# Down products of a hybrid encoder block by Strassen over two blocks and three parts of K, with operands made ahead in DRAM

## The chip, the cores and the metric

The kernel runs on one core of a Trainium2 chip. TensorE (PE) multiplies, VectorE (DVE) and ScalarE (ACT) do the elementwise work, GpSimd (POOL) mostly starts DMAs here, and SyncE (SP) starts the other DMAs. The metric is the device time of one execution in microseconds (us). The profile is a recording of one execution.

## The reference

One layer of an encoder over 2048 tokens of 1024 channels. The part that matters here is the SwiGLU at the end and the last norm:

```python
x = x + jnp.concatenate([y_a, y_b.astype(y_a.dtype)], axis=-1) @ w_out[l]
h2 = rmsnorm(x, norm2_g[l])
x = x + (jax.nn.silu(h2 @ w_gate[l]) * (h2 @ w_up[l])) @ w_down[l]
return rmsnorm(x, final_norm_g)
```

w_gate and w_up are 1024 x 2816, w_down is 2816 x 1024, everything is float32. Ahead of it stand the projections, gated linear attention in both directions, a gMLP mixer and the output projection.

## The kernel before

Activations lie as channels x tokens: 128 partitions of one channel block by 512 tokens (a block b, four of them, TB = 512). A float32 product is made of three fast ones: each operand is split into a high half, rounded by a cast on ScalarE, and a low half, the difference, on VectorE; then high x high, high x low and low x high are summed in PSUM. In program text the halves end in h and l.

The gate and up products already use the Winograd form of Strassen's method: two blocks of tokens (a pair, `PAIRS`: blocks 3 and 2, then 1 and 0), two output tiles of 128 channels (a step p, 11 of them for gate and 11 for up) and two halves of K form a 2x2 problem, done in seven products of 4 x 3 matmuls instead of eight. The seven moving operands (`slots`) are made once per pair by `moving` and `put`; the seven stationary ones are made from the raw weights for each step p by `Stationary.job`: sums of quarters of the weight on L343, a cast on L361, the low half on L362. `Stream` makes them four products ahead. `STEADY` is the order of the seven products; `quarter` is called when one of the four output tiles is complete. For gate it applies tanh on ScalarE (L968) and a product on VectorE (L969); for up it multiplies with the gate (L980) and GpSimd writes the result to DRAM (`da`, L981).

The down stage, from L1008 on, is not in that form. For each of the four blocks it loads 22 blocks of w_down (`wdn`, 512 KB each, in every block again) and 22 of the activations (`ar`), splits both (L1038, L1039 and `split`), and sums 22 x 3 products into each of 8 output tiles (`pd`, on L110 to L112). After a block the residual is added (L1097), the squares are summed, one wide sum over channels (L197) and its root give the norm, and the scaled block leaves from GpSimd's queue (L1050, L1053). The last block is done in two half columns, so that the first half's norm lies beside the second half's products; its outputs leave from SP's queue (L1107, L1110).

Instructions are written in program order, but a scheduler of the framework then sets the order on each engine from its own estimates, and may draw an instruction ahead of others of the same engine. Buffers are tiles of pools: a new tile waits until the one in its place has been read. Every engine works through its own instructions strictly in that order; a waiting instruction holds those behind it.

Of the kernel before, what the change touches and what calls it, by code (L numbers as in the profile page):

```python
# [8 lines left out]
F32 = mybir.dt.float32  # L9
# [5 lines left out]
P = 128  # L15
T = 2048
D = 1024
# [10 lines left out]
def encoder_block(  # L28
# [22 lines left out]
    wdn: bass.AP,  # L51
# [174 lines left out]
    def put(i, src):  # L226
# [3 lines left out]
        for k in range(0, HK, 2):  # L230
            c = slice(k, k + 2)
            nc.scalar.copy(out=hi[:, c, :], in_=src[:, c, :])
            nc.vector.tensor_tensor(out=lo[:, c, :], in0=src[:, c, :], in1=hi[:, c, :].bitcast(F32), op=ALU.subtract)
            yield

    def moving(b11, b21, b12, b22):
# [3 lines left out]
        def sub(o, a, b):  # L240
            for k in range(0, HK, 2):
                c = slice(k, k + 2)
# [11 lines left out]
        yield from put(6, b22)  # L254
        yield from sub(b21, b21, b11)
        yield from put(5, b21)

# [4 lines left out]
    d_a = {b: [drp.tile([P, TB], F32, tag=f"da{b}_{j}", name=f"da{b}_{j}") for j in range(NF)] for b in range(NB)}  # L262
# [15 lines left out]
    STEADY = (0, 4, 3, 1, 2, 6, 5)  # L278
# [12 lines left out]

    class Stationary:


        def __init__(self):
# [4 lines left out]
            for n, (i, p, w, o) in enumerate(self.seq):  # L300
                turn = p in (0, 1, NP - 1)
                need = []
                for r in ((0,) if o in (0, 4) else (1,) if o in (3, 5) else (0, 1)):
# [14 lines left out]
            self.stream = Stream([lambda n=n: self.job(n) for n in range(len(self.seq))], ahead=4)  # L318

        def ask(self, done):  # L320

            for x, q in enumerate(self.queues):
                while self.asked[x] < len(q) and (self.asked[x] < 2 or q[self.asked[x] - 2]["last"] < done):
# [5 lines left out]
                    self.asked[x] += 1  # L329

# [556 lines left out]


    psums.close()
    psf = ctx.enter_context(tc.tile_pool(name="psf", bufs=1, space=bass.MemoryType.PSUM))  # L890
    cg = gp.tile([P, 4, TB], F32, tag="g", name="cg")
    with tc.tile_pool(name="pf", bufs=1) as pf:
# [3 lines left out]
        slots.update({i: tuple(pf.tile([P, HK, TB], F32R, tag=f"s{i}{x}", name=f"s{i}{x}") for x in "hl") for i in (2, 5)})  # L896
        s5h, s5l = slots.pop(5)
        homes[6] = lambda: (ps6.tile([P, HK, TB], F32R, tag="w0", name="s6h"), s5l)
        homes[5] = lambda: (s5h, ps6.tile([P, HK, TB], F32R, tag="w1", name="s5l"))
        later = []  # L900

        def flush():
            while later:
                later.pop(0)()

        def seven(quarter, name):

            bank = {}

            def temp(n, bufs=2):  # L910
                return pf.tile([P, TB], F32, tag=n, name=f"{n}{name}", bufs=bufs)

            def product(i, key, start=True):
                whi, wlo = ws.next()
                if start and ops.n <= 5:
                    bank[key] = other(f"{name}{key}")
                elif start:
                    bank[key] = psf.tile([P, TB], F32, tag="sp", name=f"{name}{key}", bufs=7)
                o = bank[key]
                thi, tlo = slots[i]  # L920
                for k in range(HK):
                    c = slice(k * P, (k + 1) * P)
                    f, l = start and k == 0, k == HK - 1
                    nc.tensor.matmul(out=o, lhsT=whi[:, c], rhs=thi[:, k, :], start=f, stop=False, skip_group_check=True)
                    nc.tensor.matmul(out=o, lhsT=whi[:, c], rhs=tlo[:, k, :], start=False, stop=False, skip_group_check=True)
                    nc.tensor.matmul(out=o, lhsT=wlo[:, c], rhs=thi[:, k, :], start=False, stop=l, skip_group_check=True)
                flush()
                return o

            def add(o, a, b):  # L930
                nc.vector.tensor_tensor(out=o, in0=a, in1=b, op=ALU.add)

            def s0():
                st["u2"] = temp("u2", 4)
                nc.scalar.copy(out=st["u2"], in_=product(0, "a"))

            def s1():
                add(st["u2"], product(1, "b"), st["u2"])
# [281 lines left out]
```

## Time and profile before

| | us |
|---|---|
| median of 3 runs | 2120.22 (2115.94 to 2120.43) |
| profiled execution | 2115.95 |
| its span, first to last instruction | 2114.3 |
| TensorE busy | 2084.4 (99%) |
| VectorE busy | 1362.9 (64%) |
| ScalarE busy | 871.6 (41%) |
| GpSimd busy | 169.6 (8%) |

The profile gives for each engine how long it was busy, in slices of the span, in groups of instructions, and as a chain from the last instruction backwards. Matmuls overlap, so that a row's duration (0.39 us) is longer than the distance from one start to the next. The gate and up stage takes the span from about 772 to 1616 us, the down stage the rest.

### The profile page before, as it was taken

The numbers are of one execution on the slowest core, as the hardware profiler recorded it, in microseconds if no ns is written. First come the engines' busy times: TensorE is split into PE (matmuls) and PEld (weight loads), VectorE is DVE, ScalarE is ACT, GpSimd is POOL, SyncE is SP. The second block draws the span as 40 slices with busy tenths as digits, with TensorE's granted clock in tenths as the row PEclk, the third lists the DMA queues.
The fourth block names the chain that finished last, engine by engine and source line by source line (L and its number), as shares of the span: only waits on it lengthen the run. The fifth ranks groups of instructions, "written<-read, shape, count | busy, mean of one in ns | idle before, by whom it ended". The sixth has DMA issues, their size and how long they took to land.

```text
span 2114.3 us, 25808 instructions
## 1 busy us (share of the span) xinstructions
PE 2084.4 (99%) x9728; PEld 1706.6 (81%) x9728; DVE 1362.9 (64%) x2134; ACT 871.6 (41%) x1473; POOL 169.6 (8%) x266
## 2 busy tenths in 40 slices
PE   8999999999999999999999999999999999999998
PEld 6787877888888878888888888888888888888887
DVE  6977666676666768676666976666666355353633
ACT  6765455464646542332233523322324333233321
POOL 0222222010110100000000000000000000000000
PEclk9999999999999999999999999999999999999999
DMA  8633244453543434222222332222225537364531
GB/s 294 204 112 130 95 140 157 138 191 113 199 173 135 149 125 149 85 73 88 80 85 75 126 144 90 73 87 80 85 75 196 170 133 245 128 219 154 175 114 40
DMA packets 94109, 281.42 MB, mean 133 GB/s; under 512 B 11680, under 2 KB 19744, under 8 KB 90784
## 3 DMA queue, kind: packets, MB, share of 16 engines
q1 hardware_dynamic: 79824, 226.81, 31.6%
q0 software_dynamic: 14016, 52.44, 6.7%
q8 instruction: 76, 1.25, 0.2%
q10 hardware_dynamic: 144, 0.52, 0.1%
q14 instruction: 49, 0.40, 0.1%
HBM read 225.20 MB, written 54.53 MB: 132 GB/s over the span
## 4 chain that ended last, share of the span: by engine, by line
PE 91%; DVE 5%; DMA 2%; ACT 2%; issue 1%; SPq 0%; POOL 0%; DVEq 0%; ACTq 0%
PE pd L111 8%; PE pd L112 8%; PE pd L110 8%; PE pout L111 3%; PE pout L112 3%; PE pout L110 3%; PE pu L112 1%; PE pu L110 1%; PE pu L111 1%; PE pg L110 1%; PE pz L110 1%; PE pg L112 1%; PE pg L111 1%; PE pz L111 1%; PE pz L112 1%; PE pv L112 1%
## 5 line engine op out<-in xcount | busy, mean ns | idle before, releaser
L981 POOL DMA_DIRECT2D da<-q x88 | 47.6, 541 | 801.7 <-DVE q L980 768.9
L968 ACT ACTIVATE th<-cg 128x512 f32<-128x512 f32 x66 | 41.5, 631 | 105.5 <-DVE cg L966 97.1
L969 DVE SCALAR_TENSOR_TENSOR cg<-th,cg 128x512 f32<-128x512 f32 x66 | 45.2, 686 | 15.6 <-ACT th L968 15.6
L848 DVE TENSOR_TENSOR xc<-pout,xc 128x512 f32<-128x512 f32 x32 | 21.9, 688 | 44.1 <-PE pout L112 43.9
L980 DVE SCALAR_TENSOR_TENSOR q<-q,cg 128x512 f32<-128x512 f32 x66 | 45.3, 686 | 0.6
L1053 POOL DMA_DIRECT2D out_dram<-xg x12 | 8.6, 717 | 368.3 <-DVE xg L1050 368.3
L545 POOL TENSOR_SCALAR qs<-QK,misc 128x128 f32<-128x128 f32 x30 | 25.6, 857 | 151.8 <-DVE QK L496 77.3
L569 DVE SCALAR_TENSOR_TENSOR sf<-sf,misc,dsb 64x128 f32<-64x128 f32 x56 | 19.9, 355 | 23.3 <-ACT dsb L559 22.7
L744 DVE SCALAR_TENSOR_TENSOR sb<-sb,misc,dsr 128x128 f32<-128x128 f32 x30 | 10.0, 344 | 36.5 <-PE pob L734 35.8
L1038 ACT CAST a_8h<-ar 128x512 fp32r<-128x512 f32 x32 | 18.7, 618 | 19.0 <-DMA ar<-da 18.9
L552 ACT COPY ot<-po 128x256 f32<-128x256 f32 x32 | 10.3, 374 | 38.6 <-PE po L549 21.9
L1125 DVE TENSOR_TENSOR xg<-pd,xg 128x256 f32<-128x256 f32 x16 | 6.8, 425 | 28.2 <-PE pd L112 27.8
L729 POOL TENSOR_SCALAR qb<-qb,misc 128x128 f32<-128x128 f32 x30 | 18.4, 624 | 80.5 <-DMA qb<-dq 66.0
L1097 DVE TENSOR_TENSOR xg<-pd,xg 128x512 f32<-128x512 f32 x24 | 16.5, 690 | 12.4 <-PE pd L112 12.4
L748 ACT ACTIVATE junk<-o 128x128 f32<-128x128 f32 x64 | 19.8, 310 | 9.8 <-issue 5.9
L1127 ACT ACTIVATE lsq<-xg 128x256 f32<-128x256 f32 x16 | 6.7, 417 | 40.9 <-DVE xg L1125 40.9
L511 PEld LDWEIGHTS sc<-QK 64*128 64x128 f32 x256 | 15.7, 187 | 8.9 <-issue 4.6
L540 PEld LDWEIGHTS po<-v,s 128*128 128x128 f32 x128 | 15.8, 191 | 8.5 <-issue 5.9
L540 PE MATMUL po<-v,s 128*128 128x128 f32 x128 | 17.7, 282 | 4.0 <-DVE s L517 4.0
L1039 DVE TENSOR_TENSOR a_8l<-ar,a_8h 128x512 fp32r<-128x512 f32 x32 | 20.8, 679 | 0.7 <-ACT a_8h L1038 0.6
L511 PE MATMUL sc<-QK 64*128 64x128 f32 x256 | 19.1, 286 | 1.9 <-DVE QK L497 1.9
L1039 DVE TENSOR_TENSOR a_0l<-ar,a_0h 128x512 fp32r<-128x512 f32 x32 | 20.5, 686 | 0.8 <-ACT a_0h L1038 0.8
(3680 smaller groups left out, 7331.9 us busy)
## 6 DMA issues: line engine op xcount, KB each, us to landing
wdn<-in_wdn_dram SPq DMA_DIRECT2D x88, 512.0 KB, 3.5
da<-q POOLq DMA_DIRECT2D x88, 256.0 KB, 2.3
ar<-da SPq DMA_DIRECT2D x88, 256.0 KB, 4.1
wo<-in_wo_dram SPq DMA_DIRECT2D x32, 512.0 KB, 4.2
xk<-in_xtok_dram SPq DMA_DIRECT2D x16, 512.0 KB, 6.4
wv<-in_wv_dram SPq DMA_DIRECT2D x16, 512.0 KB, 3.5
xc<-in_xT_dram SPq DMA_DIRECT2D x4, 2048.0 KB, 9.2
wg<-in_wg_dram SPq DMA_DIRECT2D x16, 512.0 KB, 3.5
```

Source lines behind the costliest of these rows:

```text
L110: nc.tensor.matmul(out=out, lhsT=whi, rhs=ahi, start=start, stop=False, **kw)
L111: nc.tensor.matmul(out=out, lhsT=whi, rhs=alo, start=False, stop=False, **kw)
L112: nc.tensor.matmul(out=out, lhsT=wlo, rhs=ahi, start=False, stop=stop, **kw)
L511: nc.tensor.matmul(out=sc[a][:, i // 2, i % 2, :], lhsT=kd[i][r, c], rhs=qd[i][r, c], start=True, stop=True)
L540: nc.tensor.matmul(out=po[hd % 2][:, hd // 2, :], lhsT=s[:, hd, :], rhs=vs[t][:, hd, :], start=hd < 2, stop=g == 0 and hd > 1)
L545: nc.gpsimd.tensor_scalar_mul(qs[:, m, :], qd[m][:, c], ech[:, m, 2 * g:2 * g + 1])
L848: nc.vector.tensor_tensor(out=xt[:, n, :], in0=p, in1=xt[:, n, :], op=ALU.add)
L968: nc.scalar.activation(out=th, in_=a, func=AF.Tanh, scale=0.5)
L969: later.append(lambda: nc.vector.scalar_tensor_tensor(out=o, in0=th, scalar=1.0, in1=a, op0=ALU.add, op1=ALU.mult))
L980: nc.vector.scalar_tensor_tensor(out=q, in0=a, scalar=0.5, in1=cg[:, 2 * m + t, :], op0=ALU.mult, op1=ALU.mult)
L981: nc.gpsimd.dma_start(out=d_a[pair[t]][2 * p + m], in_=q)
L1039: nc.vector.tensor_tensor(out=lo, in0=raw, in1=hi.bitcast(F32), op=ALU.subtract)
```

## The change

The down products take the Winograd form too: a pair of blocks, two output tiles (q, four of them) and K in three parts of 8, 8 and 6 blocks (`PARTS`, each part halved). Results of the parts add up in SBUF (`acc`). The stationary operands of the down stage are the same for both pairs; `make_down` makes both halves of them during 12 of the 22 steps of the gate and up stage and writes them to DRAM (`d_w`), and the down stage loads them ready (`fetched`). `make_down` works in the 2 MB tile `x2`, with two buffers for high halves and one for the low half. The activations of a part are loaded by GpSimd's queue and made into the seven moving operands by `moving`. Gate uses ScalarE's Silu instead of Tanh and a product. Product 5 is done ahead of 6, here and in gate and up. In the last part of a pair the products that end the first block are done first, and its norm and output are written between the others.

```diff
-        yield from put(6, b22)
         yield from sub(b21, b21, b11)
         yield from put(5, b21)
+        yield from put(6, b22)
...
-    STEADY = (0, 4, 3, 1, 2, 6, 5)
+    STEADY = (0, 4, 3, 1, 2, 5, 6)
...
+    PARTS = (HK, HK, NF // 2 - 2 * HK)
+    DOWN = [(c, q, o) for c in range(len(PARTS) - 1) for order in (STEADY[:2], STEADY[2:])
+            for q in range(KT // 2) for o in order]
+    DOWN += [(len(PARTS) - 1, q, o) for order in ((0, 4), (1, 2, 5)) for q in range(KT // 2) for o in order]
+    DOWN += [(len(PARTS) - 1, q, o) for q, o in ((0, 3), (1, 3), (0, 6), (2, 3), (1, 6), (3, 3), (2, 6), (3, 6))]
...
+        def fetched(self, j):
+            if j % 2 == 0:
+                self.two = [wp.tile([P, D], F32, tag="w" + x, name=f"dn{self.n}{x}") for x in "hl"]
+                w = PARTS[DOWN[j][0]] * P
+                for t, d in zip(self.two, d_w[j // 2]):
...
+                    nc.sync.dma_start(out=t, in_=d)
...
-                nc.scalar.activation(out=th, in_=a, func=AF.Tanh, scale=0.5)
-                later.append(lambda: nc.vector.scalar_tensor_tensor(
-                    out=o, in0=th, scalar=1.0, in1=a, op0=ALU.add, op1=ALU.mult))
+                nc.scalar.activation(out=o, in_=a, func=AF.Silu)
...
+        def make_down(c, q, name):
+            room = xp.tile([P, KT, TB], F32, tag="x2", name=name).rearrange("p k t -> p (k t)")
+            ra, rb, sm = room[:, 0:2 * w], room[:, D:D + 2 * w], room[:, 2 * D:2 * D + w]
+            *his, lo = (room[:, 2 * D + k * TB:2 * D + k * TB + w] for k in (1, 2, 3))
...
+            def low(o, src, hi):
+                nc.vector.tensor_tensor(out=lo.bitcast(F32R), in0=src, in1=hi, op=ALU.subtract)
+                j = PLACE[c, q, o]
+                for x, d in zip((hi, lo), d_w[j // 2]):
+                    nc.gpsimd.dma_start(out=d[:, j % 2 * TB:j % 2 * TB + w], in_=x)
...
+            for o in STEADY:
+                how = {3: (sm, rb[:, c1], rb[:, c2], ALU.add), 1: (sm, sm, ra[:, c1], ALU.subtract),
+                       2: (rb[:, c1], ra[:, c1], rb[:, c1], ALU.subtract), 6: (sm, ra[:, c2], sm, ALU.subtract)}.get(o)
+                if before:
+                    low(*before)
+                if how:
+                    src = how[0]
+                    nc.vector.tensor_tensor(out=how[0], in0=how[1], in1=how[2], op=how[3])
...
+                nc.scalar.copy(out=hi.bitcast(F32R), in_=src)
...
+        def acts(c, pair):
+            hk, both = PARTS[c], []
+            for b, tag in zip(pair, ("x2", "x")):
+                t = xp.tile([P, KT, TB], F32, tag=tag, name=f"ac{b}_{c}")
+                for k in (0, hk):
+                    nc.gpsimd.dma_start(out=t[:, k:k + hk, :], in_=d_a[b][c][:, k:k + hk, :])
...
+        spans = [(0, p) for p in range(3, 8)] + [(1, p) for p in range(2, 9)]
...
+        def rstd(t, name):
+            for k in range(TT):
+                nc.tensor.matmul(out=m[:, k:k + 1], lhsT=total[t][:, k * P:(k + 1) * P], rhs=ones[:, 0:1], start=True, stop=True)
+            nc.scalar.activation(out=rc, in_=m[:, 0:TT], func=AF.Sqrt, bias=eps, scale=1.0 / D)
+            nc.vector.reciprocal(out=rc, in_=rc)
...
+            nc.tensor.matmul(out=m, lhsT=ones, rhs=total[t], start=True, stop=True)
+            nc.scalar.copy(out=total[t], in_=m)
...
-            for j in range(len(first), NF - EDGE):
-                units[j] = ws.next()
-                for n in range(KT):
-                    mms(n, [j], units)
...
+                for n, (q, o) in enumerate((q, o) for x, q, o in DOWN if x == c):
+                    sets[q][o]()
+                    if n < 10:
+                        drain(operands, 1)
...
+        rstd(1, f"{pair[1]}")
+        for q in Q:
+            leave(pair[1], 1, q, nc.sync)
```

Two places show how this moves instructions. The first is VectorE in gate step 4 of the first pair. In the kernel before, L931 adds a product to the set's sums (`u2g`, `vvg`), L362 makes low halves of weights (`op..l`), L343 sums quarters of weights, L966 and L969 finish gate tiles (`cg`). In square brackets stand the engines or DMA queues whose event an instruction waits for:

```order
L931 TENSOR_TENSOR u2g_4_7913<-g_4b,u2g_4_7913 128x512 [waits PE_49]
L362 TENSOR_TENSOR op64l<-wu_4a,op64h 128x512 [waits Activation_49]
L362 TENSOR_TENSOR op64l<-sum_8011,op64h 128x512 [waits Activation_49]
L343 TENSOR_TENSOR wg_5b<-wg_5a,wg_5b 128x512 [waits DMAHW0_49,DVE_49]
L931 TENSOR_TENSOR vvg_4_8005<-g_4d,u2g_4_7913 128x512 [waits DVE_49,PE_49]
L343 TENSOR_TENSOR sum_8011<-sum_8011,wu_4a 128x512 [waits DVE_49]
L966 TENSOR_TENSOR cg<-g_4c,vvg_4_8005 128x512 [waits DVE_49]
L969 SCALAR_TENSOR_TENSOR cg<-th_4_1_8007,cg 128x512 [waits Activation_49]
L966 TENSOR_TENSOR cg<-g_4c,u2g_4_7913 128x512 [waits PE_49]
```

In the changed kernel the same stretch, a little later in it, reads as follows; `mk_3` is the fourth piece that `make_down` makes, L1025 its low halves and L1038 its sums, L389 and L370 are the old L362 and L343, L993 the old L966, and DMASW are the events of GpSimd's DMAs:

```order
L1025 TENSOR_TENSOR mk_3_8534<-mk_3_8534 128x512 [waits DMASW3_49,Activation_49]
L993 TENSOR_TENSOR cg<-g_4e,vvg_4_8018 128x512 [waits PE_49]
L389 TENSOR_TENSOR op66l<-sum_8022,op66h 128x512 [waits DVE_49,Activation_49]
L389 TENSOR_TENSOR op66l<-wu_4b,op66h 128x512 [waits Activation_49]
L370 TENSOR_TENSOR sum_8022<-wu_4a,sum_8022 128x512 [waits DVE_49]
L1038 TENSOR_TENSOR mk_3_8534<-mk_3_8534 128x512
L993 TENSOR_TENSOR cg<-g_4c,u2g_4_7925 128x512 [waits PE_49]
L1025 TENSOR_TENSOR mk_3_8534<-mk_3_8534 128x512 [waits DMASW6_49]
L1038 TENSOR_TENSOR mk_3_8534<-mk_3_8534 128x512 [waits DVE_49]
L389 TENSOR_TENSOR op68l<-wu_4b,op68h 128x512 [waits PE_49,Activation_49]
L389 TENSOR_TENSOR op68l<-sum_8022,op68h 128x512 [waits Activation_49]
L1025 TENSOR_TENSOR mk_3_8534<-mk_3_8534 128x512 [waits DMASW7_49,Activation_49]
```

The products with `th` are gone, and between the others stand the new piece's sums and low halves, the latter waiting for GpSimd's DMAs. Of this piece's seven low halves the distances, counted in instructions, are 8, 7, 4, 5, 4 and 10, and 9 to the first of the next piece.

The second place is the end of VectorE's instructions. In the kernel before, L1125 adds the last products (`pd`) to the residual, and what stands behind them is the second half column's norm:

```order
L1125 TENSOR_TENSOR xg_15394<-pd_6_15513,xg_15394 128x256 [waits PE_49]
L1125 TENSOR_TENSOR xg_15394<-pd_7_15527,xg_15394 128x256 [waits PE_49]
L1117 RECIPROCAL rl<-rl 128x128 [waits Activation_49]
L1117 RECIPROCAL rl<-rl 128x128
L1107 SCALAR_TENSOR_TENSOR xg_15394<-xg_15394,gfs,rl 128x256 [waits DVE_49]
L1107 SCALAR_TENSOR_TENSOR xg_15394<-xg_15394,gfs,rl 128x256 x7
```

In the changed kernel L1116 adds products (`d_2_3c`, part 2 of K, tile pair 3) and squares (`sq`) to their sums (`acc`, `tot`), L1132 and L1133 are the norm, L1142 scales:

```order
L1116 TENSOR_TENSOR tot_13229<-sq_1_2_0_16206,tot_13229 128x512 [waits Activation_49]
L1116 TENSOR_TENSOR acc_13227<-d_2_3c,acc_13227 128x512 [waits PE_49]
L1116 TENSOR_TENSOR tot_13229<-sq_1_3_0_16219,tot_13229 128x512 [waits Activation_49]
L1132 RECIPROCAL rc_16222<-rc_16222 128x4 [waits Activation_49]
L1133 TENSOR_TENSOR tot_13229<-ident,rc_16222 128x512 [waits DVE_49,PE_49]
L1142 SCALAR_TENSOR_TENSOR acc_13224<-acc_13224,gfs,tot_13229 128x512 [waits Activation_49]
L1142 SCALAR_TENSOR_TENSOR acc_13224<-acc_13224,gfs,tot_13229 128x512
L1142 SCALAR_TENSOR_TENSOR acc_13225<-acc_13225,gfs,tot_13229 128x512 x2
L1142 SCALAR_TENSOR_TENSOR acc_13226<-acc_13226,gfs,tot_13229 128x512 x2
L1142 SCALAR_TENSOR_TENSOR acc_13227<-acc_13227,gfs,tot_13229 128x512 x2
```

Behind the last product now stand whole 512-wide operations where half-wide ones stood.

## Rows read from the trace of the kernel before

**Rows 1.** The page: busy time by engine, granted clock in 40 slices.

```profile
PE 2084.4 (99%) x9728; PEld 1706.6 (81%) x9728; DVE 1362.9 (64%) x2134; ACT 871.6 (41%) x1473; POOL 169.6 (8%) x266
...
PEclk9999999999999999999999999999999999999999
```

**Rows 2.** Waits of TensorE, 772 to 1616: engine, line, releaser: us, times, longest.

```profile
PE g_1a L924 <- ACT op2h L361: 1.8, 1, 1.8
```

**Rows 3.** Waits of TensorE, 1616 to the end.

```profile
PE flm L1143 <- ACT lsq L1127: 1.0, 1, 1.0
```

**Rows 4.** Timeline of TensorE, start of the down stage: start us, duration us, operation.

```profile
1616.84 0.39 PE L110 MATMUL pd<-a_0h,wdn_0h 128*128 128x512 f32 x1
...
1629.76 0.39 PE L110 MATMUL pd<-a_0h,wdn_2h 128*128 128x512 f32 x1
...
1635.19 0.39 PE L110 MATMUL pd<-a_0h,wdn_3h 128*128 128x512 f32 x1
```

**Rows 5.** The chain that ended last, in order of time: start us, duration us.

```profile
115.05 1.13 PE po L540 x8
...
1862.70 0.86 PE f2m L197 x2
1983.28 0.86 PE f1m L197 x2
```

**Rows 6.** Timeline of all engines at the end of the kernel.

```profile
2103.49 0.28 PE L112 MATMUL pd<-a_16h,wdn_21l 128*128 128x256 f32 x1
...
2107.78 3.26 DVE L1107 SCALAR_TENSOR_TENSOR xg<-xg,gfs,rl 128x256 f32<-128x256 f32 x8
```

**Rows 7.** Stretches: length, busy by engine (instructions), clock, DMA share, GB/s.

```profile
core 0: us, PE busy (x) PEld busy (x) DVE busy (x) ACT busy (x) POOL busy (x), PEclk, DMA share, GB/s
...
1000.00:1076.00 76.00, 76.00 (x333) 61.54 (x332) 49.47 (x79) 22.49 (x39) 4.18 (x8) 1.00 0.23 83
...
1740.00:1860.00 120.00, 120.00 (x529) 99.02 (x528) 58.28 (x71) 42.01 (x54) 2.88 (x4) 1.00 0.53 179
```

**Rows 8.** Timeline of VectorE in gate step 6; in brackets its idle time before.

```profile
1013.07 0.69 DVE L343 TENSOR_TENSOR sum<-wg_7b 128x512 f32<-128x512 f32 x1 [2.29 <-DMA wg_7b<-in_wgu_dram]
1013.68 0.68 DVE L931 TENSOR_TENSOR u2g<-g_6b,u2g 128x512 f32<-128x512 f32 x1
...
1017.28 0.68 DVE L966 TENSOR_TENSOR cg<-g_6c,vvg 128x512 f32<-128x512 f32 x1
```

**Rows 9.** The up result `q`: durations min/median/max in ns, then its DMA's landing.

```profile
L981 POOL DMA_DIRECT2D da<-q x88: 540/542/552, 788.5 to 1618.7; - x88
L980 DVE SCALAR_TENSOR_TENSOR q<-q,cg x66: 680/684/693, 810.1 to 1617.8; 128x512 f32<-128x512 f32 x66
...
DMA to landing us min/median/max: 2.3/2.3/4.9
```

**Rows 10.** DMA issues: line's tensors, queue, count, KB each, median us to landing.

```profile
wdn<-in_wdn_dram SPq DMA_DIRECT2D x88, 512.0 KB, 3.5
da<-q POOLq DMA_DIRECT2D x88, 256.0 KB, 2.3
...
out_dram<-xg POOLq DMA_DIRECT2D x12, 512.0 KB, 4.1
...
out_dram<-xg SPq DMA_DIRECT2D x8, 256.0 KB, 2.3
```

**Rows 11.** Costliest groups by line: busy us, mean ns, idle time before and releasers.

```profile
L968 ACT ACTIVATE th<-cg 128x512 f32<-128x512 f32 x66 | 41.5, 631 | 105.5 <-DVE cg L966 97.1 <-issue 8.4
...
L1050 DVE SCALAR_TENSOR_TENSOR xg<-xg,gfs,r 128x512 f32<-128x512 f32 x24 | 16.1, 745 | 0.0
...
L198 ACT ACT_TABLE_LOAD x5 | 6.4, 1283 | 0.1
```

**Rows 12.** The mixer's tile `u`: VectorE's subtraction while GpSimd computes, ns.

```profile
L705 DVE TENSOR_TENSOR y2l<-u,y2h x4: 693/1286/1297, 468.8 to 489.2; 128x512 fp32r<-128x512 f32 x4
```

More of the change, by code (lines that the diff above doesn't have):

```diff
@@ L906, in seven @@
[L906 to L938, printed above, removed]
-            def s2():
-                d = product(2, "d")
-                st["vv"] = temp("vv")
-                add(st["vv"], d, st["u2"])
-                quarter(1, 1, bank["c"], st["vv"])
-            def s3():
-                product(3, "c")
-            def s4():
-                quarter(0, 0, product(4, "a", False), None)
-            def s5():
-                quarter(1, 0, product(5, "e"), st["vv"])
-            def s6():
-                quarter(0, 1, product(6, "c", False), st["u2"])
-            st = {}
-            return dict(enumerate((s0, s1, s2, s3, s4, s5, s6)))
@@ L994, in encoder_block @@
             sets[i, p, w][o]()
+            if (i, p) in spans:
+                turn += 1
+                if turn == 14:
+                    drain(makes)
+                elif turn % 2 == 0 or turn > 10:
+                    drain(makes, 1)
             if i == 0 and p < 2:
                 drain(operands, 1)
-            elif i == 0 and p == 2 and o == STEADY[0] and w == 0:
+            elif i == 0 and p == 2:
                 drain(operands)
+            elif i == 0 and p == 3:
+                drain(norm, 1)
+            elif i == 0 and p == 8 and (w, o) == (0, STEADY[0]):
+                drain(norm)
@@ L1006, in encoder_block @@
                 drain(operands, 1)
                 done += 1
-            flush()
+            elif i == 1 and p == 9 and (w, o) == (0, STEADY[0]):
+                operands = acts(0, PAIRS[0])
+            elif n > last[1] + 1:
+                drain(operands, 1)
     with tc.tile_pool(name="pg", bufs=1) as pg:
-        order = PAIRS[0] + PAIRS[1]
-        count = [0, 0]
-        def scratch(name):
-            return pg.tile([P, TB], F32, tag="sq", name=name, bufs=2)
-        def down_unit(b, j):
-            i = count[0]
-            count[0] += 1
-            pool, tag, bufs = (wp, "w", None) if i % 8 < 3 else (pg, "dw", 5)
-            raw = wp.tile([P, D], F32, tag="wraw", name=f"wdn{b}_{j}", bufs=2)
-            nc.sync.dma_start(out=raw, in_=wdn[j])
-            return split(pool, raw, [P, D], tag, f"wdn{b}_{j}", bufs)
@@ new lines, in encoder_block, with temp, add @@
+        halves = []
+        def temp(n, bufs):
+            if n == "vv":
+                return pg.tile([P, TB], F32, tag="vv", name="vvd", bufs=1)
+            if not halves:
+                t = wp.tile([P, D], F32, tag="wraw", name="u2d", bufs=2)
+                halves.extend((t[:, 0:TB], t[:, TB:D]))
+            return halves.pop(0)
+        def add(o, a):
+            nc.vector.tensor_tensor(out=o, in0=a, in1=o, op=ALU.add)
+        acc = [(pg if q else gp).tile([P, 4, TB], F32, tag=f"acc{q}" if q else "g", name=f"acc{q}") for q in range(KT // 2)]
@@ L1153, in _arrange @@
+        rstd(1, f"{pair[1]}")
+        for q in Q:
+            leave(pair[1], 1, q, nc.sync)
+        assert not later
 def _arrange(inp):
```

306 lines of the change are left out of this document (169 added, 137 removed).

## The prediction, made before the changed kernel was run

> **What bounds the kernel now.** I read the page first: TensorE is busy for 99% of the span at the full granted clock, VectorE for 64% [rows 1]. Busy matmuls can still wait, so the waits of TensorE come next: between 772 and 1616 us it waits for another engine once, 1.8 us, and from 1616 to the end once, 1.0 us [rows 2, 3]. So time goes or comes where the number of products changes, or where a new wait reaches TensorE. The timeline gives the pace: two products 24 apart start 5.43 us apart [rows 4], and in the chain two sums over channels, with 528 products and one such sum of 0.86 us between them, stand 120.58 us apart [rows 5], which makes (120.58 - 0.86) / 528 = 0.2267 us a product. The down stage runs from 1616.84 [rows 4] to the last product at 2103.49, which ends its turn at 2103.6 [rows 6]: 486.8 us. What follows, to 2114.3, is a tail of 10.7 us.
>
> **Down products.** Before, 22 blocks of K times 8 output tiles times 3 passes times 4 blocks are 2112 products of 512 columns (192 half ones stand for 96 of them). After, two pairs times 4 tile pairs times 7 products times 11 blocks of K times 3 passes are 1848; the gate and up stage keeps its 3696. 1848 x 0.2267 = 418.9 us. Into this stream come three norms (the fourth is in the tail), each of four narrow sums and a wide one. The narrow ones are not in the trace; the nearest row has eight products of 128 columns in 1.13 us [rows 5], so 0.6 us for four; with 0.86 us for the wide one that is 1.4 us each and 4.3 us for three. The new stage is 423.2 us if nothing waits: **63.6 us less**.
>
> **Tail.** Before, the last half column block goes through add, square, sum, root, reciprocals, eight 256-wide scalings in 3.26 us, and the last 256 KB leave 3.3 us after them [rows 6]. After, the second block of the pair has its whole norm behind the last product: add 0.69, square 0.63, add 0.69, five sums 1.4, root of four columns under 0.5, reciprocal under 0.3, product with the identity 0.69, copy 0.63, eight 512-wide scalings at about 0.7 (0.745 for one alone) = 5.6, and 512 KB out, 3.3 + 0.8 = 4.1 (0.26 MB at 338 GB/s, below); 128x512 operations are those of [rows 8, 11]. That is 15.2 us, so **+4.5 us**, between +3 and +6.
>
> **Making the operands beside gate and up.** In 12 of the 22 steps over p a piece of w_down is loaded, formed into seven operands, split and written out. Per step VectorE gains 7 subtractions and 4 sums, and loses 4 products through Silu and the plain multiply: 47 instructions instead of 40. Packed, six instructions take 3.60 us [rows 8], 0.60 each, so 28.4 us of the 38.1 us that 168 products take (now 24.7 [rows 7]). ScalarE gains 7 casts at 0.63 on 11 us, GpSimd 14 issues at 0.54 on 2 [rows 7, 9, 11]; both stay under half and are hidden. Silu is not in the trace; the Tanh beside it takes 0.63 us [rows 11] and I take that for it, with ScalarE's idle half as the cover. Its table loads, 1.28 us each, lie under the same cover.
> The new wait is the low half: there is one buffer for it, so each subtraction on L1025 waits until the DMA of the one before has landed, and behind it on VectorE stand the halves for the next products. On SP the piece's two loads wait for the last landing of the piece before, with the weights of gate and up behind them; VectorE waits 2.29 us for such a weight now and TensorE does not [rows 8], since the halves are four products, 10.9 us, ahead. The same 10.9 us cover every single wait below. By the order shown, 8, 7, 4, 5, 4 and 10 instructions lie from one such subtraction to the next and 9 to the next piece. With a landing time of L, a round trip is 0.69 + 0.1 + L against 0.605 per instruction; at the piece's change it is 0.69 + L, 3.5 us for the next load [rows 10], a cast and some 0.3, against 5.4. A landing of 256 KB takes 2.3 us now, 4.9 at most [rows 9], but at 83 GB/s [rows 7]; a step would now move 7.9 MB, 206 GB/s. The nearest row at such a load is the output's 512 KB from the same queue, 4.1 us [rows 10]. At L = 2.3 the waits add up to 3.4 us, VectorE to 31.8 of 38.1: no loss. At 4.1 they are 11.3, 39.7 of 38.1, and 12 steps lose 19 us. I take 3.3, halfway, since half as many bytes travel: 7.4 us of waits, 35.8 of 38.1, which fits on average but not in every step; **+6 us**, ends 0 and 19.
> The load rule of the Trainium skill (DMA: Bandwidth & Descriptors, section "Latency and other measured facts") is that an HBM access costs 0.2 us on average and 2 us under high load. As an estimate from that page the landing would become 2.3 + 1.8 = 4.1 us, so by it the step loses the 19 us; the trace shows both 2.3 and 4.1 us, in different stages.
>
> **Feeding the down stage.** The operands come back from DRAM: 512 KB per 12 products, 193 GB/s. With the activations (23 MB), x and the output it is 121 MB in 423 us, 285 GB/s. Before, this stage moves 179 GB/s at a DMA share of 0.53 [rows 7], so 338 at full share: 84%. Three pairs of operand tiles keep two pairs ahead, 10.9 us. The 4.2 MB of activations for the next part are 12.4 us of all engines; if they went wholly ahead of the operands, 1.5 us would be missing, five times 8 us. In the last part of the first pair VectorE has 50 adds and squares' sums, 8 scalings, and some 20 us of operand work, 57 us in 57 us of products; a few us may wait there. Below, nothing: **+4 us**, ends 0 and 12. Slot 5 ahead of 6 changes no count and no duration: 0, because the sums it needs are formed four products ahead either way.
>
> **Sum.** Against the profiled execution, 2115.95 us (2114.3 and 1.65 around it): 2115.95 - 63.6 + 4.5 + 6 + 4 = 2066.9. That execution was as fast as the fastest of the three timed ones, 2115.94, and 4.3 under their median, 2120.22; I add half of that: **2069 us**.
>
> **Rivals.**
> *The low half's round trip becomes the pace, and the kernel slower.* Place: L1025 in the 12 steps. The other terms leave 55 us of gain, 4.6 a step, so it decides from waits of 14.3 us a step, L = 4.6. At 4.9, the longest landing of this queue's 256 KB, the waits are 16.1, a step 44.5, and 12 of them lose 77: 2138 us. For it: one buffer, seven trips in a row, 2.5 times the traffic. Against: the median is 2.3, and the 512 KB take 4.1 at nearly that load.
> *The same, milder:* L near 4.1 and the feeding at its upper end, +19 and +12: 2088 to 2092 us.
> *DMA sets the pace of the down stage.* At 262 GB/s instead of 285 its 121 MB take 460 us, 37 more: 2104. For it: 84% on average with bursts. Against: two pairs of slack, and this queue mix ran at 338 GB/s at full share.
> *VectorE and GpSimd block one another.* When GpSimd computes beside it, a VectorE subtraction of two SBUF tiles takes 1.29 us instead of 0.69 [rows 12]. If each of the 14 new issues cost 0.6 us, a step would be 28.4 + 8.4 + 7.4 = 44.2 and the kernel 73 us longer, 2134. Against: beside the 88 issues of now the products on L980 take 680 to 693 ns, and the issues 540 to 552 [rows 9].
> That is a rule of the Trainium skill (SBUF — State Buffer, section "Who interferes with whom"): a VectorE instruction with two SBUF inputs contends with a GpSimd instruction that reads SBUF. For tensor operations rows 12 agree with it; for DMA issues rows 9 show no such cost.
>
> **How the numbers follow.** Forecast 0.78 (2055 to 2082); milder round trip 0.12; DMA pace 0.05; the two that end slower 0.05. The low end is every wait at nothing: 2115.95 - 63.6 + 3 = 2055. The high end takes in the milder case with the median's share: 2095. Within 0.2% (4 us, about what a measurement here can tell from no change) lies only a thin strip between the DMA case and the slow ones: 0.01. Faster 0.94, slower 0.05.
>
> **What would show it.** Right: TensorE's groups of the down stage take some 423 to 430 us and its waits stay under 12 us in all; gate and up still end near 1617 to 1630; the tail from the last product is near 15 us. The landing of the low halves reads about 3.3 us, and VectorE's idle time before L1025 is put down to that DMA, some 5 to 8 us a step. Wrong: TensorE waiting for halves from L389 in every step (round trip), for d_w tiles in the down stage (DMA pace), or VectorE's 128x512 operations well above 0.69 us while GpSimd issues. If the granted clock falls below full in the stretches with waits, the loss is larger than any term above.

## The result, and the profile after

The changed kernel takes 2147.39 us (median of four runs, 2141.12 to 2156.6) against 2120.32 for the kernel before, run beside it: 1.0136 times as long, interval 1.0095 to 1.0176. The forecast was 2069 (2055 to 2095) and faster: the direction is wrong and the miss is 78 us. The profiled execution took 2156.6 us, 9.2 over the median; its own time is what the profile explains.

A stage is measured here from the start of its first product to that of the next stage's first, on TensorE's timeline.

| us, profiled execution | before | forecast | after |
|---|---|---|---|
| gate and up | 848.6 | 854.6 | 892.9 |
| down stage, to the end of the last product | 486.8 | 427.2 | 474.3 |
| tail | 10.7 | 15.2 | 17.7 |

First TensorE's busy time and clock on the page of the changed kernel (before: [rows 1]):

```profile
PE 2058.5 (96%) x9384; PEld 1669.9 (77%) x9384; DVE 1468.8 (68%) x2294; ACT 862.6 (40%) x1485; POOL 287.1 (13%) x486
...
PEclk9999999999999999999999999999999999999998
```

The work went down as counted (2084.4 to 2058.5 busy, although the slower products are counted in it), but the share fell from 99% to 96%: TensorE now waits. Its waits, first in gate and up (before: 1.8 us, [rows 2]); columns are the engine and line, the releaser, us in all, times, longest:

```profile
PE g_2a L932 <- ACT u2g L942: 4.9, 2, 3.1
PE g_5c L932 <- DVE cg L993: 4.4, 2, 2.7
PE g_2c L932 <- ACT mk L1042: 4.0, 1, 4.0
PE g_3c L932 <- DVE cg L993: 3.0, 2, 2.4
PE g_4c L932 <- DVE cg L993: 2.7, 2, 2.1
...
PE u_5c L932 <- DVE q L1003: 2.5, 1, 2.5
...
PE g_1a L932 <- ACT op2h L388: 1.9, 1, 1.9
```

and then from there to the end (before: 1.0 us, [rows 3]):

```profile
PE d_0c L932 <- DVE acc L1116: 9.1, 1, 9.1
PE d_3a L932 <- DMA dn370h<-dw31h: 5.8, 1, 5.8
PE d_0c L934 <- DMA dn316l<-dw4l: 3.0, 1, 3.0
...
PE fr L1137 <- DVE tot L1133: 1.5, 1, 1.5
```

The fourteen rows of gate and up add to 33.7 us, the thirteen of the down stage ahead of the tail to 31.6. No row names a half of gate's and up's weights but one of 1.9 us that was there before. In gate and up 26.7 us of it are at a bank `c`, which VectorE has not read yet (the row that names ScalarE's `mk` belongs to them: VectorE's read of the bank ended at 872.45, that cast at 872.51, the product began at 872.60); in the down stage 21.8 are at operands that have not landed.

The waits don't cover the whole loss, 44.3 us in gate and up. A look at stretches around the 4.0 us wait shows the rest (columns as in [rows 7]; the seventh value is the granted clock):

```profile
868.30:872.60 4.30, 0.35 (x2) 0.03 (x1) 4.30 (x8) 1.68 (x4) 1.21 (x3) 0.84 0.38 150
872.60:876.60 4.00, 4.00 (x10) 3.13 (x11) 2.95 (x5) 2.61 (x5) 1.59 (x3) 0.50 0.51 173
...
881.00:890.00 9.00, 9.00 (x41) 7.28 (x40) 6.56 (x10) 2.97 (x6) 2.16 (x4) 1.00 0.49 178
```

After the wait ten products take 4.0 us, at the lower of the two clock levels (0.50, 1.2 GHz); a row counts what touches its stretch, and 41 touch 9.0 us at the full one. So 44.3 less 31.9 us of added waits leaves some 12 us. By the distances from one product to the next, about 10 of them are products that run slowly after a wait. The first row shows one thing more: during this longest wait VectorE was busy for all of the 4.30 us. It had stood idle for 4.71 us at a low half some ten us earlier, and what was held up there then ran one behind the other.

**Gate and up, one wait.** VectorE's timeline in gate step 4 (in brackets its idle time and what ended it), then TensorE's:

```profile
951.10 0.69 DVE L1025 TENSOR_TENSOR mk<-mk 128x512 fp32r<-128x512 f32 x1 [2.89 <-ACT mk L1042]
951.71 0.68 DVE L938 TENSOR_TENSOR u2g<-g_4b,u2g 128x512 f32<-128x512 f32 x1
...
954.11 0.68 DVE L938 TENSOR_TENSOR vvg<-g_4d,u2g 128x512 f32<-128x512 f32 x1
...
955.31 0.68 DVE L993 TENSOR_TENSOR cg<-g_4c,vvg 128x512 f32<-128x512 f32 x1
```

```profile
951.18 0.39 PE L932 MATMUL g_4e<-s5h,op60h 128*128 128x512 f32 x1
...
956.13 0.47 PE L932 MATMUL g_4c<-s6h,op62h 128*128 128x512 f32 x1 [2.07 <-DVE cg L993]
```

Product 6 adds to bank `c`, which L993 has to read first, and L993 needs the sums of products 1 and 2 before it. Product 2 ends when 5 starts, at 951.18; 5 lasts twelve matmuls, 2.72 us. The last sum `vvg` and L993 are 1.2 us of that, so VectorE may be 1.5 us late and no more. It stood at a low half of the new operands for 2.89 us, with the gate's sums behind; this time for a cast on ScalarE, which had stood for the piece's load. Over the 84 low halves and casts (busy us, mean ns, idle time before them and what ended most of it):

```profile
L1025 DVE TENSOR_TENSOR mk<-mk 128x512 fp32r<-128x512 f32 (+1 forms) x84 | 54.1, 644 | 78.8 <-ACT mk L1042 19.1 <-DMA dw15l<-mk 9.3 <-DMA dw36l<-mk 5.6
...
L1042 ACT CAST mk<-mk 128x512 fp32r<-128x512 f32 (+1 forms) x84 | 47.9, 584 | 119.7 <-DVE mk L1025 27.9 <-DMA mk<-in_wds_dram 25.6 <-DVE mk L1038 13.2
```

and the last line of the view on the tile `mk`, the landing of the new piece's transfers:

```profile
DMA to landing us min/median/max: 2.1/2.8/9.1
```

VectorE's 78.8 us are 6.6 a step, of which 59.3 in all (4.9 a step) ended when a low half before had landed and 19.1 (1.6 a step) with a cast. The landing has a median of 2.8 us over all the pieces' transfers (the low halves alone: 2.5, mean 3.1). ScalarE, too, stands at casts of the piece until its loads and VectorE's sums have come, and with it the copy L942 that the row on `u2g` names.

**Down stage.** Landing of DMAs issued between 1670 and 1690, during the first part (count, KB each, median us to landing), with the share of each queue:

```profile
DMA packets 1735, 7.64 MB, mean 382 GB/s; under 512 B 241, under 2 KB 241, under 8 KB 1366
...
q0 software_dynamic: 1053, 5.10, 68.6%
q1 hardware_dynamic: 681, 2.52, 32.0%
...
acc<-dx POOLq DMA_DIRECT2D x11, 256.0 KB, 13.6
...
dn316l<-dw4l SPq DMA_DIRECT2D x1, 512.0 KB, 13.6
```

In calm stretches such an operand lands in 3.1 to 4.2 us; here GpSimd's queue moves two thirds of the bytes, and it takes 13.6, past the 10.9 us of cover. Besides the next part's activations (4 MB) the residual is loaded there, 2.8 MB. At the change of the pair something else happens, on GpSimd, ScalarE and VectorE:

```profile
1933.27 0.56 POOL L1054 DMA_DIRECT2D ac<-da  x1
1941.76 1.07 POOL L1123 DMA_DIRECT2D acc<-dx  x2 [7.92 <-DMA out_dram<-acc]
1942.82 1.58 POOL L1054 DMA_DIRECT2D ac<-da  x3
```

```profile
1945.38 1.99 ACT L233 CAST tah<-ac 128x1024 fp32r<-128x1024 f32 x2 [19.41 <-DMA ac<-da]
```

```profile
1946.45 1.23 DVE L234 TENSOR_TENSOR tal<-ac,tah 128x1024 fp32r<-128x1024 f32 x1 [9.40 <-ACT tah L233]
```

The first load of the activations `ac` is issued at 1933.27, behind loads of the residual that had waited 4.6, 1.2 and 1.2 us for outputs to leave, and lands at 1945.36, 12.1 us later. ScalarE's cast waits for it, VectorE stands at the first subtraction, and behind that stand the sums that free TensorE's bank: the 9.1 us. The other three loads are later still, behind a residual that waits 7.92 us until the output before it has left.

**Tail.** The second sum over channels runs at a low clock, and takes 2.04 us for its two passes, where two at full clock are 0.86 ([rows 5]):

```profile
2142.45 2.04 PE L1137 MATMUL fr<-tot,ones 128*128 128x512 f32 x2 [1.46 <-DVE tot L1133]
```

### The profile page after: what moved, and what is told of

It is laid out like the page before. It is cut to its first block, busy times and chain, and to the rows that moved or that the text cites. A ratio compares the mean times of both kernels' runs of the same rounds, so it can differ in the third digit from the quotient of the medians.

```text
span 2154.9 us, 25682 instructions
## 1 busy us (share of the span) xinstructions
PE 2058.5 (96%) x9384; PEld 1669.9 (77%) x9384; DVE 1468.8 (68%) x2294; ACT 862.6 (40%) x1485; POOL 287.1 (13%) x486
## 3 DMA queue, kind: packets, MB, share of 16 engines
q0 software_dynamic: 32000, 122.18, 15.1%
## 5 line engine op out<-in xcount | busy, mean ns | idle before, releaser
L1025 DVE TENSOR_TENSOR mk<-mk 128x512 fp32r<-128x512 f32 (+1 forms) x84 | 54.1, 644 | 78.8 <-ACT mk L1042 19.1
L1042 ACT CAST mk<-mk 128x512 fp32r<-128x512 f32 (+1 forms) x84 | 47.9, 584 | 119.7 <-DVE mk L1025 27.9
L995 ACT ACTIVATE cg<-cg 128x512 f32<-128x512 f32 x66 | 41.5, 631 | 113.6 <-DVE cg L993 113.4
L1005 DVE TENSOR_TENSOR q<-q,cg 128x512 f32<-128x512 f32 x66 | 45.2, 685 | 0.1
L1156 ACT ACTIVATE sq<-acc 128x512 f32<-128x512 f32 x28 | 17.7, 632 | 65.6 <-DVE acc L1116 62.2
L234 DVE TENSOR_TENSOR tal<-ac,tah 128x1024 fp32r<-128x1024 f32 (+1 forms) x24 | 26.7, 1131 | 23.6 <-ACT tah L233 23.6
L1038 DVE TENSOR_TENSOR mk<-mk 128x512 f32<-128x512 f32 (+1 forms) x48 | 30.8, 643 | 1.8 <-DMA mk<-in_wds_dram 1.1
L1116 DVE TENSOR_TENSOR acc<-vvd,acc 128x512 f32<-128x512 f32 x48 | 31.0, 686 | 0.5
L234 DVE TENSOR_TENSOR tbl<-ac,tbh 128x1024 fp32r<-128x1024 f32 (+1 forms) x24 | 26.9, 1129 | 6.4 <-ACT tbh L233 6.4
L244 DVE TENSOR_TENSOR ac<-ac 128x1024 f32<-128x1024 f32 (+1 forms) x24 | 26.9, 1128 | 1.7 <-DMA ac<-da 1.7
L244 DVE TENSOR_TENSOR ac<-ac,ac 128x1024 f32<-128x1024 f32 (+1 forms) x24 | 26.6, 1129 | 0.1
L579 ACT COPY ot<-po 128x256 f32<-128x256 f32 x32 | 10.3, 373 | 39.5 <-PE po L576 21.7
L1142 DVE SCALAR_TENSOR_TENSOR acc<-acc,gfs,tot 128x512 f32<-128x512 f32 x32 | 21.9, 745 | 5.8 <-ACT tot L1138 5.8
```

Of the source, the lines that this page charges most:

```text
L244: nc.vector.tensor_tensor(out=o[:, c, :], in0=a[:, c, :], in1=b[:, c, :], op=ALU.subtract)
L995: nc.scalar.activation(out=o, in_=a, func=AF.Silu)
L1005: nc.vector.tensor_tensor(out=q, in0=a, in1=cg[:, 2 * m + t, :], op=ALU.mult)
L1025: nc.vector.tensor_tensor(out=lo.bitcast(F32R), in0=src, in1=hi, op=ALU.subtract)
L1038: nc.vector.tensor_tensor(out=how[0], in0=how[1], in1=how[2], op=how[3])
L1042: nc.scalar.copy(out=hi.bitcast(F32R), in_=src)
```

## The experiments

Each table row is a kernel run beside the kernel before (ratio to it with its interval); the stages are those of its profiled execution. Between profiled executions of the same code a stage differs by some 5 us (e1, e2, e5 to e9 and e12 leave the down stage as it was: 470.7 to 476.1), so the verdicts on a few us go by the medians. The changed kernel's own median is known to about 9 us (its interval), so a difference from it is known no better; the other medians are known to about 2 to 4 us.

| | median | ratio | gate and up | down |
|---|---|---|---|---|
| after | 2147.39 | 1.0136 (1.0095 to 1.0176) | 892.9 | 474.3 |
| e1_lo2 | 2145.08 | 1.0125 (1.0108 to 1.0143) | 880.7 | 473.5 |
| e2_room | 2152.33 | 1.0161 (1.0148 to 1.0174) | 889.1 | 474.6 |
| e3_spread | 2130.45 | 1.0047 (1.0030 to 1.0064) | 888.8 | 451.4 |
| e4_both | 2130.92 | 1.0051 (1.0038 to 1.0065) | 890.7 | 452.1 |
| e5_nomake | 2109.94 | 0.9955 (0.9940 to 0.9970) | 845.8 | 474.0 |
| e6_nodma | 2122.01 | 1.0011 (1.0001 to 1.0020) | 860.9 | 472.2 |
| e7_slack | 2134.07 | 1.0065 (1.0048 to 1.0081) | 873.9 | 475.8 |
| e8_pace | 2124.03 | 1.0024 (1.0013 to 1.0035) | 861.0 | 476.1 |
| e9_pace2 | 2126.80 | 1.0037 (1.0024 to 1.0051) | 863.6 | 476.1 |
| e10_full | 2094.86 | 0.9883 (0.9870 to 0.9896) | 862.8 | 441.4 |
| e11_full_slack | 2082.63 | 0.9826 (0.9812 to 0.9840) | 851.7 | 440.6 |
| e12_pace_only | 2128.84 | 1.0042 (1.0029 to 1.0056) | 866.2 | 470.7 |
| e13_best | 2082.39 | 0.9821 (0.9807 to 0.9834) | 851.6 | 444.3 |

**e1_lo2 and e2_room: take away the waits at the low half.** The first theory was that these waits alone are the loss of gate and up.

```diff
-            *his, lo = (room[:, 2 * D + k * TB:2 * D + k * TB + w] for k in (1, 2, 3))
+            his = [room[:, 2 * D + k * TB:2 * D + k * TB + w] for k in (1, 2, 3)]
...
+                lo = pf.tile([P, TB], F32, tag="lo", name=f"lo{name}_{o}", bufs=2)[:, 0:w]
```

> Edit: the low half of a piece of w_down gets two buffers of its own instead of one, and the high half three instead of two; the same instructions and bytes. Theory (the loss in gate and up, 892.7 us instead of 848.4, comes from VectorE standing at L1025 until a DMA of a half has landed, with the quarter add L993 behind it that frees the PSUM bank for product 6): L1025's idle time falls from 78.8 us to under 30, TensorE's waits for L993 and L1003 under 10 us in all, gate and up to 855 to 870 us, the kernel to 2110 to 2125. Rival (the seven more VectorE instructions and the DMA bytes of a step are the cost themselves): the waits at L1025 fall, the stage stays above 885 us and the kernel within 6 us of 2147.

e2 has, further, `lo = src if o in (2, 5, 6)` and one `room` for all pieces of a pair.

> Edit: as the two buffers, and three of the seven low halves are written over the sum that they come from, which nothing reads later; all pieces of a pair share one tile, so that the next piece's loads wait only for the part they overwrite. Theory (waits at L1025 and at the change of the piece): L1025's idle time under 15 us, gate and up 850 to 860 us, the kernel 2100 to 2112. Rival (the piece's change does not matter): the same as with two buffers within 4 us. Rival (work and bytes are the cost): stage above 885 us.

The theory fell. VectorE's idle time at the low halves went from 78.8 to 36.9 us, and the kernel gained nothing that can be told (2145.08). The trace of e1 says why. The low halves of the changed kernel, those of e1 with the landing of their DMAs, and a stretch of e1:

```profile
L1025 DVE TENSOR_TENSOR mk<-mk x84: 549/684/695, 804.7 to 1485.3; 128x512 fp32r<-128x512 f32 x56, 128x384 fp32r<-128x384 f32 x28
```

```profile
L1026 DVE TENSOR_TENSOR lomk<-mk x84: 548/685/694, 803.7 to 1395.0; 128x512 fp32r<-128x512 f32 x56, 128x384 fp32r<-128x384 f32 x28
...
DMA to landing us min/median/max: 2.1/3.6/7.8
```

```profile
1270.00:1395.00 125.00, 111.11 (x457) 88.82 (x456) 95.56 (x162) 48.82 (x93) 45.10 (x84) 0.95 0.67 234
```

The last low half is at 1395.0, in the changed kernel at 1485.3: with a buffer free, the order draws the pieces further ahead of their steps, and up to 14 low halves stand in one step instead of up to 10. In that stretch VectorE is at 76%, the DMA at 0.67, and TensorE has 111 of 125 us. The low halves now land in 3.6 us at the median (2.5 before), and ScalarE still stands 31.7 us at casts until a high half before has landed (36.5 in the changed kernel, 42.3 in e2). e2 does the same with less idle time still (30.0 us at the low halves), and is, if anything, slower.

**e3_spread and e4_both: the loads of the activations.**

```diff
+            def loads():
+                for k in (0, hk):
+                    for t, b in zip(both, pair):
+                        (eng or nc.gpsimd).dma_start(out=t[:, k:k + hk, :], in_=d_a[b][c][:, k:k + hk, :])
+                        yield
...
+                    elif n in (11, 14, 17, 20):
+                        drain(pieces, 1)
```

> Edit, in the down stage alone: the four 1 MB loads of the next part's activations go to SyncE's queue, one after every third product, between the loads of the operands, instead of all four at once on GpSimd's queue; the same bytes. Theory (the bursts on the second queue stretch the operands' landing past 10.9 us, and at the pair's change the activations stand behind the residual loads that wait for the output): TensorE's waits for dn tiles fall from some 23 us to under 6, the 9.1 us at the pair's change go, the down stage falls from 474 to 435 to 448 us, the kernel to 2108 to 2122. Rival (285 GB/s is too much on average, whenever the bytes come): the waits move to other products, the stage stays above 465 us.

> Edit: the shared tile with low halves in place and two buffers, and the spread loads, together. If the two losses are independent: 2147 less what each gave alone, about 2065 to 2085, 35 to 55 us below the kernel before. If they share a cause (the granted clock, or the DMA as a whole): less than nine tenths of the sum.

The stage falls from 474.3 to 451.4, a little less than written down, and the kernel by 16.9 us by the medians, not to 2122; the wait of 9.1 us is gone (four of 4.5 in all are left there). The waits for operands fall from 21.8 to 10.0 us, not under 6, since the first burst stayed: `dn316l` still lands in 14.5 us beside six residual loads on GpSimd's queue. e4 gains no more than e3, because e2's part is no gain; its forecast rested on the theory that fell. Against e2 alone the loads bring 21.4 us. The edit changes several things at once, the queue, the spreading, and the time of the loads (one product later for the first, ten for the last), and no run takes them apart.

**e5_nomake and e6_nodma: what does the making cost?**

```diff
-                makes, turn = make_down(*x, f"mk{x[0]}_{x[1]}"), 0
+                makes, turn = make_down(*x, f"mk{x[0]}_{x[1]}") if x == (0, 0) else None, 0
...
-                for x, d in zip((hi, lo), d_w[j // 2]):
+                for x, d in zip((hi, lo), d_w[j // 2] if (c, q) == (0, 0) else ()):
```

(the first edit is e5's, the second e6's; in both, L351's `d_w[j // 2]` becomes `d_w[0]`)

> Left out: of the twelve pieces of w_down only the first is made and written; the down stage loads that one pair of halves for every product (same bytes, wrong operands). The rest of gate and up, with Silu and the new order of slots, is as in the changed kernel. If making the operands is the whole loss of that stage: gate and up 848 to 853 us instead of 892.7, the kernel 2103 to 2110. If Silu in place of tanh and product, or slot 5 ahead of 6, costs by itself: above 860 us.

> Left out: the pieces are loaded and made on VectorE and ScalarE as in the changed kernel, but only the first is written to DRAM; the down stage loads that one for every product. So no buffer waits for a DMA, and 154 issues on GpSimd and 75 MB of traffic go. If the work on VectorE and the order in which it is drawn in are the cost: gate and up stays above 872 us. If the waits for the halves' landing, or GpSimd's issues and the traffic, were the cost (the two extra buffers would then have moved the waits only): under 860 us.

Without the pieces the stage takes 845.8 us, less than before the change, so Silu and the order of the slots cost nothing. Making is the whole loss of gate and up: 37.5 us by the medians. Without the writes 25.4 of them go, and VectorE's and ScalarE's work is left with 12.1 us; the stage, 860.9, lies at the edge of the range written down for the waits and the traffic. The order packs the work even more here, up to 17 low halves in one step:

```profile
L1025 DVE TENSOR_TENSOR mk<-mk x84: 550/684/697, 804.6 to 1367.2; 128x512 fp32r<-128x512 f32 x56, 128x384 fp32r<-128x384 f32 x28
```

So the packed work alone, without writes to wait for, costs little.

**e7_slack: give VectorE a later deadline.**

```diff
+            for n in range(6, len(one) - 7, 7):
+                one[n], one[n + 1] = one[n + 1], one[n]
```

> Edit: product 6 of a set is issued one product later, behind the next set's product 0, in the steady steps of gate and up; the same products. Theory (TensorE waits because VectorE has 2.72 us after product 2 to read bank c, of which two instructions take 1.2, and any delay over 1.5 us at VectorE becomes a wait of TensorE): the quarter add gets 5.44 us, most waits of 1 to 3 us go, gate and up 855 to 872 us instead of 892.7, the kernel 2115 to 2130. Rival (VectorE cannot carry the step's work, so a later deadline only defers the wait): above 885 us, the waits move to other lines.

13.3 us by the medians, the stage 873.9, just outside the ranges written down: the bank's deadline is a mechanism of the loss, but not all of it; what is left stands at the next set's product 0, behind ScalarE's copy.

```profile
PE g_3a L935 <- ACT u2g L945: 3.8, 1, 3.8
```

**e8_pace, e9_pace2 and e12_pace_only: keep each piece in its step.**

```diff
+            nc.scalar.copy(out=ra[:, 0:1], in_=u2[:, 0:1])
             for x, r in ((ra, 0), (rb, 1)):
```

`u2` is what product 0 of the gate step leaves, so the piece's loads can't be ordered before it. e8 is this on e2, e12 on the changed kernel; e9 adds to e8 a copy into the first high half ahead of the first cast.

> Edit, on the version with the shared tile: a one-column copy on ScalarE into the piece's tile, which reads what product 0 of the step leaves, stands ahead of the piece's loads, so that the order cannot draw a piece ahead of its step: about 7 low halves a step in 12 steps, instead of up to 14 in 9 steps there and up to 10 in the changed kernel. If the packing into few steps is what the shared tile's version lost (888.9 us): gate and up 855 to 868 us, the kernel 2112 to 2125. If each piece costs its 3 to 4 us wherever it lies: above 880 us.

> Edit, on the changed kernel alone: the one-column copy on ScalarE ahead of a piece's loads, so that no piece is drawn ahead of its step; one low buffer, two high ones and a tile per piece as before. If the single low buffer's round trip costs by itself: gate and up 875 to 893 us against 860.8 with pacing, more buffers and the shared tile. If the clustering into few steps is all: within 4 us of 860.8.

> Edit, on the paced version: the piece's loads start at the step's product 0, its first cast and with it the first low half only after product 1, four products (10.9 us) later, held by a second one-column copy on ScalarE into the first high half. Theory (what is left of the loss is VectorE standing at the piece's second operand until its load has landed, 1.2 to 2.5 us a step): those waits go, gate and up 849 to 855 us instead of 860.8, the kernel 2110 to 2118. Rival (the eleven VectorE instructions themselves): gate and up stays above 858.

Pacing alone gains 18.6 us, with the single low buffer left in place (e12; its stage, 866.2, lies between the two ranges), and with more buffers 23.4 (e8), 28.3 against e2: nearly what leaving the writes out gains. So the clustering was the larger part; what the buffers add to it, 4.8 us by the medians, is hardly clear of noise. With e6 this says more: packed work without its writes costs 12.1 us, spread work with its writes 14.1 (e8 over e5), so it is packed work together with its writes that costs. The waits for their landing are the likely way: at casts, until a high half has landed, ScalarE stands 36.5 us in the changed kernel and 2.9 in e8. That the traffic has no part of its own in it is not shown. The stretch of e1 above, in e8, with VectorE at 71% and TensorE at 120.68 of 125:

```profile
1270.00:1395.00 125.00, 120.68 (x521) 97.89 (x520) 88.91 (x143) 48.44 (x87) 28.77 (x54) 0.99 0.53 188
```

The low halves then hold VectorE for 4.6 us in all, where e12, with one buffer, has 38.4. e9's theory fell: its first cast comes later, but VectorE stands at the piece's sums as before (31.8 us in e8, of which 23.3 until a load of w_down has landed; 28.8 and 21.7 in e9). In e11, SyncE's timeline shows one of the reasons, the load of the second operand issued right behind a weight of gate:

```profile
954.16 0.33 SPq L1022 DMA_DIRECT2D mk<-in_wds_dram  x1
954.58 0.50 SPq L346 DMA_DIRECT2D wu_5b<-in_wgu_dram  x1
969.29 0.33 SPq L346 DMA_DIRECT2D wg_6a<-in_wgu_dram  x1
969.71 0.94 SPq L1022 DMA_DIRECT2D mk<-in_wds_dram  x1
```

That load comes 15.6 us after the first operand's. It was not moved to another queue in a run.

**e10_full, e11_full_slack and e13_best: all together.** On e9, e10 has the loads of e3, and the first pair's residual on SyncE's queue too; e11 adds e7's edit; e13 is e11 without e9's copy.

```diff
-            nc.gpsimd.dma_start(out=acc[q][:, 2 * t + m, :], in_=d_x[b][:, 2 * q + m, :])
+            eng.dma_start(out=acc[q][:, 2 * t + m, :], in_=d_x[b][:, 2 * q + m, :])
```

> Edit: the paced and held pieces, the activations of the next part one by one on SyncE's queue, and the residual of the first pair there too, between the operands' loads. If the gains add up: gate and up 849 to 855, the down stage 440 to 451, the kernel 2082 to 2098, the first version under the kernel before. If the residuals at the first part's start were no part of the operands' lateness: the down stage stays at 451.

> Edit: as the one before, and product 6 of a set one product later in gate and up. If single waits of 1 to 2 us are left at bank c in gate and up: 3 to 8 us less than the version without. If none is left: the same within 3 us, or a little more, since the next set's product 0 needs its bank earlier.

> Edit: paced pieces with buffers and shared tile, without the held first cast; product 6 one product later; activations and the first pair's residual on SyncE's queue. If the hold is worth nothing beside the later product 6: within 4 us of 2082.6. If VectorE's wait for the piece's second operand is shorter without the hold (1.2 to 2.5 us instead of 3.9 to 4.9) and the later product 6 covers it: 2074 to 2080.

e10 is 1.2% faster than the kernel before, with the down stage as written down and gate and up at 862.8 instead of 849 to 855; e11 and e13 are 1.7 and 1.8% faster (36.5 and 36.7 us), 65 us under the changed kernel. With the residual among the operands on one queue the operand above lands in 6.1 us (13.6 in the changed kernel):

```profile
dn316l<-dw4l SPq DMA_DIRECT2D x1, 512.0 KB, 6.1
```

The later product 6 brings 12.2 us more, above what was written down; the held cast nothing beside it. The three stages of e13:

```profile
772.00:1622.20 850.20, 842.49 (x3694) 694.94 (x3693) 638.35 (x986) 329.69 (x573) 139.95 (x260) 1.00 0.44 155
1622.20:2066.50 444.30, 433.39 (x1879) 348.47 (x1877) 294.14 (x390) 103.45 (x136) 15.02 (x25) 1.00 0.71 254
2066.50:2084.20 17.70, 3.44 (x11) 1.67 (x10) 8.12 (x13) 1.48 (x3) 0.00 (x0) 0.60 0.31 119
```

## Why the prediction was wrong

The miss against the profiled execution is 89.7 us: making the operands +38.3, feeding the down stage +47.1, the tail +2.5 (its five sums take 3.1 us at a granted clock of 0.62, 1.4 was put down), and 1.8 by which gate starts later (770.0 against 768.2, in code that did not change).

- **The count of products** is right. TensorE has 1848 in the down stage, and e11 with few waits left takes 440.6 us for them and the norms, 17 over the 423.2 without any.
- **Making, +6: this step failed**, at the sentence "The same 10.9 us cover every single wait below". The size of VectorE's waits came out near: 6.6 us a step against 7.4 worked out, at a landing of 2.8 us against 3.3, though 1.6 of the 6.6 are waits for casts. But the halves for the next products are not the only thing behind VectorE that TensorE waits for. The deadline is bank `c`: 2.72 us, of which 1.5 are free. e7, which doubles it, shows that it counts. The trace of the kernel before has the same distance and could have told: in gate step 4 product 5 starts at 938.20 and product 6 at 940.84, with VectorE's add on L966 from 940.10 to 940.78 between them.
- **The sum over a mean step** failed with it. The prediction counts 47 instructions for each of 12 even steps, and found them to fit on average. The order had drawn up to 10 low halves into one step. e8 and e12 show the price: 18.6 to 28.3 us for keeping about seven in a step. It is the price of a packed step with its writes, not of its instructions alone, since e6 packs up to 17 without writes and loses 12.1 us.
- **ScalarE "hidden at under half"** is the same mistake on another engine: it was idle enough, but in order, and its copy L942 stood behind casts of the piece.
- **Feeding, +4: this step failed too.** The bytes were about right (113.7 MB between 1660 and 2137, against 121 worked out), the burst was not: the prediction puts 4.2 MB of activations ahead of the operands and finds 1.5 us missing, five times. There were 2.8 MB of residual in the first burst besides, landings of 13.6 us, and waits of 3 to 8 us at four places, each with slow products behind it. The 9.1 us at the pair's change, an activation load held on GpSimd's queue by residuals that wait for outputs, and then 12.1 us to its landing, were in no case of it. e3 and e10 give 23 and then 10 us of the stage back.
- **The clock** was named as what would make the loss larger than any term, but had no price. It is some 12 us in gate and up and, with the norms' longer sums, up to 19.5 in the down stage (51.1 us over the pace, less 31.6 of waits).
- **Silu and the slots** cost nothing, as said: 845.8 us without the pieces. **GpSimd's issues** don't slow VectorE, as said: L1025 takes 684 ns at the median beside 168 new ones.
- **The rivals.** The slower side had 5 in 100. Its first mechanism, a landing over 4.6 us that paces VectorE, is not what happened: 2.8 us was enough, because the cover was 1.5 us and not 10.9. The rival on DMA's pace fell: the average fits, as e10 shows by moving the same bytes in 441.4 us with 3.7 us of waits for operands.

What stays open: which of VectorE's or ScalarE's instructions hold the 12.1 us that are left without the writes (by the stage, 15.1 us over e5's in e6 and 5.9 in e11, which has the later deadline); what of e3's gain is the queue and what the later, spread loads; and the price of the clock by itself, since no run here holds it.

## What to carry to other kernels

For work put beside a full TensorE, look for the shortest deadline, not the usual one: of all that stands behind a waiting instruction on its in-order engine, find the PSUM bank or tile that TensorE needs first, and compare each single wait with that. A mean per step says little where an order may draw work ahead; count the fullest step with its transfers, and if a buffer that throttles is taken away, put a dependence on TensorE's own progress in its place. Transfers that are small on average did better here between the urgent ones on one queue than in a block on another.

## What the runs showed of the hardware

Two DMA queues at work share the engines: between 1670 and 1690 GpSimd's queue had 68.6% of their time and SyncE's 32.0%, and a 512 KB load on SyncE's took 13.6 us instead of 3.1 to 4.2. The Trainium skill (DMA: Bandwidth & Descriptors, section "Queues, rings and completion order") says that each engine takes turns between the queues that have work, packet by packet; the trace agrees in that neither queue stands still, though it does not show the packets' turns.

A TensorE wait can cost more than its length: after one of 4.0 us the granted clock was 0.50 for the next 4.0 us, in which ten products ran instead of some eighteen at 0.2267 us. Not every wait does: after one of 2.7 us, which ended at 1442.96, it stayed at 1.00, and 18 products touch the next 4.0 us.
